# Stick-breaking attention: low key parts on 128 rows, paired products with v, and an earlier third key projection

## The chip, the core and the metric

The kernel runs on one core of a Trainium2 chip. The core has a matrix engine, TensorE (PE in the profile; its loads of the stationary operand are listed apart as PEld), two elementwise engines, VectorE (DVE) and ScalarE (ACT), the slower GpSimd (POOL), and a sync engine (SP) that issues the DMAs. Matmuls read SBUF and write PSUM, which has eight banks of 128 rows by 512 fp32 numbers. The metric is the device time of one execution, in microseconds (us); the median of several runs counts.

## What is computed

The reference is an encoder of two layers on 512 tokens of width 1024. Each layer has a feed-forward block, a token mixer, a second feed-forward block and a gated embedding. The mixer is what the change touches. It projects its input once (`h @ w_in`) and feeds three branches: a stick-breaking attention of four heads of 64, a gated delta rule of four heads of 128 in chunks of 64 tokens (its queries, keys and values pass a convolution over four tokens and a silu), and a short convolution.

```python
def stick_breaking_attention(q, k, v):
    ...
        z = jnp.einsum('bhqd,bhkd->bhqk', qb, kp) * scale
        mask = jnp.arange(t1)[None, :] < jnp.arange(t0, t1)[:, None]
        log_skip = jnp.where(mask, jax.nn.log_sigmoid(-z), 0.0)
        later = lax.cumsum(log_skip, axis=3, reverse=True) - log_skip
        att = jnp.where(mask, jnp.exp(jax.nn.log_sigmoid(z) + later), 0.0)
        outs.append(jnp.einsum('bhqk,bhkd->bhqd', att, vp))
    ...
def gated_delta_rule_chunked(q, k, v, g, beta):
    ...
    gcum = jnp.cumsum(g, axis=-1)
    decay = jnp.exp(jnp.where(incl, gcum[..., :, None] - gcum[..., None, :], -jnp.inf))
    k_beta = k * beta[..., None]
    m = jnp.where(strict, jnp.einsum('nbhik,nbhjk->nbhij', k_beta, k) * decay, 0.0)
    t_inv = lax.linalg.triangular_solve(eye + m, ...)
    ...
```

## The kernel before

**Precision.** Large products run in fp16 in three matmuls: each operand is split into a high part (a rounded copy, made by ACT) and a low part (the rest, made by DVE). `mm3` (lines 256 to 258) issues high by high, high by low and low by high. `split_part` (lines 139 and 140) splits a weight; `load_cols` fetches 256 columns of a weight matrix by one DMA (line 148) and splits them in two halves. Smaller products run directly in fp32; each such matmul shows two records in the profile.

**Order.** The program is written down in one sequence, and a planner makes from it a fixed order for each engine: what stands earlier goes first, but where by the planner's estimates an instruction isn't ready, a later one that is ready fills the gap. So projections written behind a stage stand among its matmuls. An engine works off its order and waits where an input isn't there. Tiles come from pools with a number of buffers per tag: `psa` has two PSUM banks (`acc`, for projections), `psb` three (`bank`), `psc` three (`bank2`); the tag `cv` has five buffers of 128x512 fp32, for convolved projections and for the attention's `l`; the tag `t2` has six.

**The mixer**, `mix_body`, in the order of the program:

- Lines 600 to 611 project the attention's values (`pv` to `sbv`).
- Lines 613 to 625: `conv` copies a projection from PSUM with the last tap (ACT, line 616) and adds three shifted taps (DVE, line 619). The keys of the delta rule come in four projections, one a head. The first two are made here and convolved (`early`).
- Lines 628 to 679 are the gates' work: the decay `g` and `beta` from eight columns, products for cumulative sums (`pe`, lines 654 to 657), their exponential `eg`, and the decay matrices `E` and `ET` (through `gm`, `pl` and `gd`).
- Lines 706 to 722: the silu of each head's keys, transposes and row sums. The weights of the third and fourth key heads are loaded at the head of the second round (lines 707 and 708), and these heads are projected and convolved there (line 711).
- Lines 739 to 789 form `M` and invert its 16x16 blocks, in many small DVE steps and by way of DRAM.
- Lines 795 to 815 project the attention's queries and keys (`psb`). `qs` and `ks` have one tile of 128 rows for each head. In `qs` the head's own 64 rows hold the high part of the queries and the other 64 the low part; `ks` holds the high part of the keys twice. So one matmul on 128 rows gives high by high and low by high. `kl` holds the low part of the keys on the own 64 rows, two heads to a tile, and the third product is a matmul on 64 rows.
- Lines 820 to 873 are the attention, twelve units (h, kts): head h with the key blocks kts, which are (2, 3), (1,) or (0,). A block k meets the queries from k*128 on: 512 columns for block 0, 384, 256 and 128 for blocks 1 to 3. A unit sets up logits in a bank `zb` (three matmuls a block, lines 830, 834 and 838, the last adding the mask), takes softplus (DVE 844, ACT 845 and 846, DVE 847), splits it (ACT 849, DVE 850), sums it over later keys by matmuls with constant triangles (line 857), takes the exponential (ACT 862), and multiplies by the values in fp32 (line 867). That product goes to 64 of the 128 rows of the bank `pav`, which two heads share. Four such groups of a double block, two groups of block 1 and two of block 0 stand alone; block 0 of heads 0 and 2 comes next to block 1 of heads 1 and 3. When both heads are done, lines 872 and 873 copy `pav` out.
- Lines 876 to 896 are the short convolution's projections (`psh`, `psc`, `psbb`); behind them come the values and queries of the delta rule (`pvv`, `pqq`), its gate (`pz`), the sequence of eight chunks, and the output projection.

Of the kernel before, what the change touches and what calls it, by code (L numbers as in the profile page):

```python
# [9 lines left out]
F16 = mybir.dt.float16  # L10
# [3 lines left out]
ALU = mybir.AluOpType  # L14
# [3 lines left out]
P = 128  # L18
D = 1024
KD = D // P  # L20
S = 512
NT = S // P
# [8 lines left out]
IWS = 1.0 / WS  # L31


class Block:
# [524 lines left out]
    def mix_body(self, i, j, last, pool):  # L559
        nc, ins, xT, x = self.nc, self.ins, self.xT, self.x  # L560
        sm = self.small
        w_in = ins["mix_w_in"][i]

        H, C, NC, G16 = 4, 64, 2 * NT, NT * 4
        halves = [slice(64 * e, 64 * e + 64) for e in range(2)]
        heads = [(hp, e) for hp in range(2) for e in range(2)]
        OFF_Q, OFF_K, OFF_V, OFF_Z, OFF_AB, OFF_SC = 768, 1280, 1792, 2304, 2816, 2824
# [20 lines left out]
        ps = self.bank2("ps_rows", (P, 64))  # L588
# [11 lines left out]
        sbv = pool.tile([P, NT, 256], F32, name="sbv")  # L600
# [12 lines left out]
        def conv(ps, c):  # L613
            a = pool.tile([P, S], F32, name="conv", tag="cv", bufs=5)
            w = lambda tap: cw[:, tap * 12 + c : tap * 12 + c + 1]
            nc.scalar.activation(a, ps, AF.Copy, scale=w(3))
            for tap in (2, 1, 0):
                d = 3 - tap
                nc.vector.scalar_tensor_tensor(
                    a[:, d:], ps[:, : S - d], w(tap), a[:, d:], op0=ALU.mult, op1=ALU.add  # L620
                )
            return a

        w = self.load_cols(w_in, OFF_K)
        early = [conv(self.proj_T(w, xT, e, "pk", self.bank2), 4 + e) for e in range(2)]
# [3 lines left out]
        for c in range(2):  # L629
            for e in range(2):  # L630
                nc.tensor.matmul(
                    pab[halves[e], :, c], self.ident[:, halves[c]], ab[:, :, e::2],
                    start=True, stop=True,
# [15 lines left out]
        nc.scalar.activation(beta, pab[:, :, 2:4], AF.Exp, scale=-1.0)  # L649
        nc.vector.tensor_scalar(beta, beta, 1.0, None, op0=ALU.add)  # L650
        nc.vector.reciprocal(beta, beta)
        g16 = g.rearrange("p n h -> p (n h)")
        pe = self.bank("pe", (P, 4, G16))
        nc.tensor.matmul(pe[:, 0], self.uin, g16, start=True, stop=True)
# [40 lines left out]
        def turn(src, name):  # L695


            pts = [self.bank(name, (P, 4, P)) for _ in range(2)]
            for n in range(NC):
                nc.tensor.transpose(pts[n // 4][:, n % 4], src(n), self.ident)  # L700
            return [(pt, slice(4 * b, 4 * b + 4)) for b, pt in enumerate(pts)]

        def chunks(v):
            return v.rearrange("p (n c) -> p n c", c=C)

        for hp in range(2):
            if hp == 1:
                w = self.load_cols(w_in, OFF_K + 256)
            for e in range(2):
                h = 2 * hp + e  # L710
                a = conv(self.proj_T(w, xT, e, "pk"), 4 + h) if hp else early[e]
                self.silu(kq[h][:, :, 0], chunks(a))
            for pt, ns in turn(lambda n: kq2[hp][:, n, 0].rearrange("p e c -> p (e c)"), "pkt"):
                sq = self.t2("sq", (P, 4, P))
                nc.scalar.activation(sq, pt, AF.Square)
                nc.vector.tensor_reduce(
                    ssk[:, ns, hp], sq, axis=mybir.AxisListType.X, op=ALU.add
                )
                nc.vector.tensor_tensor(
                    kdec[:, ns, hp], pt, bc(eg[:, 1].rearrange("p (n h) -> p n h", h=2)[:, ns, hp]),  # L720
                    op=ALU.mult,
                )
# [18 lines left out]
        for a in range(2):  # L741
            a8 = slice(8 * a, 8 * a + 8)
            pm = self.bank("pm", (P, 4, 2, C))
            for n in range(4):
                for hp, e in heads:
                    ks = kq[2 * hp + e][:, 4 * a + n, 0]
# [47 lines left out]

        qs = pool.tile([P, H, S], F16, name="qs", tag="m4", bufs=4)
        ks = pool.tile([P, H, S], F16, name="ks", tag="m4", bufs=4)
        kl = self.t2("kl", (P, 2, S), F16)
        rows_of = lambda e: slice(64 * e, 64 * e + 64)
        for hp in range(2):
            ps = self.proj_T(wq, xT, hp, "psb")  # L800
            for e in range(2):
                own, other, h = rows_of(e), rows_of(1 - e), 2 * hp + e
# [4 lines left out]
        for hp in range(2):  # L807
            ps = self.proj_T(wk, xT, hp, "psb")
            for e in range(2):
                own, other, h = rows_of(e), rows_of(1 - e), 2 * hp + e  # L810
                nc.scalar.activation(ks[own, h], ps[own], AF.Copy, scale=IWS)
                nc.vector.tensor_copy(ks[other, h], ks[own, h])
                nc.vector.scalar_tensor_tensor(
                    kl[own, hp], ps[own], IWS, ks[own, h], op0=ALU.mult, op1=ALU.subtract
                )
        mT = self.act.tile([P, 2, KD, S], F16, name="mT", tag="xT", bufs=2)
        hlb = self.w1.tile([P, 4, 2, 512], F16, name="hl", tag="w")
        pav, hls = [None] * 2, [[None] * NT for _ in range(H)]

        for n_u, (h, kts) in enumerate(((0, (2, 3)), (0, (1,)), (1, (2, 3)), (0, (0,)), (1, (1,)), (2, (2, 3)),  # L820
                       (1, (0,)), (2, (1,)), (3, (2, 3)), (2, (0,)), (3, (1,)), (3, (0,)))):
            hp, e = divmod(h, 2)
            es = slice(64 * e, 64 * e + 64)
            off = {k: 256 * (k == 3) for k in kts}
            n = 512 if kts == (0,) else 384
            zb = self.bank2("zb")[:, :n]
            zt = {k: zb[:, off[k] : off[k] + S - k * P] for k in kts}
            for k in kts:
                kc = slice(k * P, (k + 1) * P)
                nc.tensor.matmul(  # L830
                    zt[k], ks[:, h, kc], qs[:, h, k * P :],
                    start=k == kts[0], stop=False, skip_group_check=True,
                )
                nc.tensor.matmul(
                    zt[k], kl[es, hp, kc], qs[es, h, k * P :], start=False, stop=False,
                    skip_group_check=True,
                )
                nc.tensor.matmul(
                    zt[k][:, :P], self.identb, self.later, start=False, stop=False,
                    skip_group_check=True,  # L840
                )
            l = pool.tile([P, 512], F32, name="sp", tag="cv", bufs=5)[:, :n]

            nc.vector.tensor_scalar(l, zb, 40.0, None, op0=ALU.min)
            self.after(nc.scalar.activation(l, l, AF.Exp), tables)
            nc.scalar.activation(l, l, AF.Ln, bias=1.0)
            nc.vector.tensor_tensor(l, zb, l, op=ALU.max)
            pair = hlb[:, n_u % 4]
            nc.scalar.activation(pair[:, 0, :n], l, AF.Copy)
            nc.vector.tensor_tensor(pair[:, 1, :n], l, pair[:, 0, :n], op=ALU.subtract)  # L850
            for k in kts:
                hls[h][k] = pair[:, :, off[k] : off[k] + S - k * P]
            for k in reversed(kts):
                for k2 in range(NT - 1, k - 1, -1):
                    lhs = self.ntri if k2 == k else self.nones
                    for q in range(2):
                        nc.tensor.matmul(
                            zt[k][:, (k2 - k) * P :], lhs, hls[h][k2][:, q], start=False,
                            stop=k2 == k and q == 1, skip_group_check=True,
                        )  # L860
            at = l
            self.tables_end = nc.scalar.activation(at, zb, AF.Exp)
            if e == 0 and kts[0] == 2:
                pav[hp] = self.bank2("pav")
            for k in kts:
                a0 = at[:, off[k] : off[k] + S - k * P]
                nc.tensor.matmul(
                    pav[hp][es, k * P :], sbv[:, k, 64 * h : 64 * h + 64], a0,
                    start=k == 2, stop=k == 0, skip_group_check=True,
                )  # L870
            if e == 1 and kts == (0,):
                nc.scalar.activation(mT[:, 0, hp], pav[hp], AF.Copy)
                nc.vector.tensor_tensor(mT[:, 1, hp], pav[hp], mT[:, 0, hp], op=ALU.subtract)

# [2 lines left out]
        hb, a = ([self.t2(n) for _ in range(2)] for n in ("hb", "sca"))  # L877
        for c in range(2):
            nc.scalar.activation(hb[c], self.proj_T(wh, xT, c, "psh"), AF.Copy, scale=IWS)
        for c in range(2):  # L880
# [3 lines left out]
            w = lambda tap: cw[:, 48 + 2 * tap + c : 49 + 2 * tap + c]  # L884
# [53 lines left out]
        for hp in range(2):  # L938
            w = self.load_cols(w_in, OFF_V + 256 * hp)
            pair = self.w1.tile([P, NC, 2, C], F32, name="vp", tag="w")  # L940
            for e in range(2):
                next(level, None)
                a = conv(self.proj_T(w, xT, e, "pvv"), 8 + 2 * hp + e)
# [6 lines left out]
        for hp in range(2):  # L950
            w = self.load_cols(w_in, OFF_Q + 256 * hp)
            for e in range(2):
                h = 2 * hp + e
                next(level, None)
                a = conv(self.proj_T(w, xT, e, "pqq"), h)
# [11 lines left out]
        for a in range(2):  # L967
            a8 = slice(8 * a, 8 * a + 8)
            pm = self.bank("pqk", (P, 4, 2, C))
            for n in range(4):  # L970
                for hp, e in heads:
                    k, q = (kq[2 * hp + e][:, 4 * a + n, s] for s in range(2))
# [7 lines left out]
        for hp in range(2):  # L980
            w = self.load_cols(w_in, OFF_Z + 256 * hp)
# [192 lines left out]
```

## Time and profile before

| | |
|---|---|
| median of three runs | 2020.03 us (2019.24 to 2020.5) |
| the profiled execution | 2017.74 us |
| its span in the profile | 2016.0 us |
| granted TensorE clock | 0.996 |
| mixer of the first layer | about 342 to 600 us of the span |
| attention of the first layer | 411.8 to 476.2 us |
| attention of the second layer | 1408.4 to 1472.8 us |

The profile shows one execution. The span runs from the first to the last instruction; the execution's own time has some 1.7 us around it. In a row of the timeline stand the start in us, the length, the engine, the line of the kernel, the operation, what it writes and reads, the form, and the number of merged instructions; in brackets stands how long the engine was idle before, and what released it. The form of a matmul gives the rows and columns of the array in use (64*128 is 64 rows and 128 columns), then the moving operand. The length of a matmul covers its way through the array, so lengths overlap, and the cost of one in a stream is the distance from its start to the next start. A weight load's row (PEld) stands apart from its matmul.

### The profile page before, as it was taken

What the parts mean: (1) busy time and instruction counts of PE and PEld (TensorE: products, weight loads), DVE (VectorE), ACT (ScalarE), POOL (GpSimd) and SP (SyncE); (2) the same over time, 40 slices, a digit from 0 to 9 for tenths busy, and PEclk for the clock granted to TensorE, in tenths of its full rate; (3) what the DMA queues carried; (4) which work ended last, traced back from release to release, by engine and by line L of the source; (5) the groups of instructions that cost most, each with busy time, mean ns of one, the idle gap of its engine ahead of it and who ended that gap; (6) DMA issues with size and microseconds to landing.
All of it is one profiled execution on the core that took longest, in us unless ns stands there. A gap on an engine that the chain in (4) does not pass through costs nothing.

```text
span 2016.0 us, 33100 instructions
## 1 busy us (share of the span) xinstructions
PE 1966.5 (98%) x14058; PEld 1274.0 (63%) x14058; DVE 1524.1 (76%) x2347; ACT 871.4 (43%) x1295; POOL 65.7 (3%) x84
## 2 busy tenths in 40 slices
PE   7999999999999999999999999999999999999998
PEld 5677686544545686776467685854455466776853
DVE  7995866765679895958897877577656797967586
ACT  6453452444345353444264453424544354443431
POOL 1000000100000000000000000001000000000000
PEclk9999999999999999999999999999999999999999
DMA  7543320420253543334224343212222624433221
GB/s 217 189 118 105 105 85 1 127 57 22 84 177 97 155 117 105 105 105 146 106 84 126 105 125 87 62 63 69 53 65 70 201 71 152 113 105 84 95 74 42
DMA packets 245359, 205.15 MB, mean 102 GB/s; under 512 B 20846, under 2 KB 225500, under 8 KB 245212
## 3 DMA queue, kind: packets, MB, share of 16 engines
q1 hardware_dynamic: 245212, 203.05, 33.1%
q8 instruction: 110, 1.80, 0.4%
q14 instruction: 37, 0.30, 0.0%
HBM read 200.14 MB, written 2.88 MB: 101 GB/s over the span
## 4 chain that ended last, share of the span: by engine, by line
PE 74%; DVE 14%; ACT 7%; DMA 2%; issue 2%; SPq 1%; POOL 0%; DVEq 0%; ACTq 0%
PE po L258 7%; PE po L256 7%; PE po L257 7%; PE pA L256 6%; PE pA L257 6%; PE pA L258 6%; DVE w L140 3%; PE pB L258 3%; PE pB L257 3%; PE pB L256 3%; DVE wq L140 2%; ACT w L139 2%; ACT wq L139 2%; PE pC L258 1%; PE pC L257 1%
## 5 line engine op out<-in xcount | busy, mean ns | idle before, releaser
L140 DVE SCALAR_TENSOR_TENSOR wq<-f,wq 128x1024 f16<-128x1024 f32 (+1 forms) x240 | 333.9, 1394 | 19.0 <-ACT wq L139 15.7
L139 ACT ACTIVATE wq<-f 128x1024 f16<-128x1024 f32 (+1 forms) x240 | 279.5, 1191 | 126.0 <-PE pB L258 83.2
L139 ACT ACTIVATE w<-raw 128x1024 f16<-128x1024 f32 (+1 forms) x196 | 193.8, 1031 | 268.2 <-PE po L258 226.1
L256 PE MATMUL po<-w,hT 128*128 128x512 f16 x704 | 266.7, 379 | 3.0 <-ACT hT L286 0.9
L256 PE MATMUL pA<-xS,wq 128*128 128x256 f16 x960 | 261.6, 273 | 6.9 <-ACT up L407 5.5
L257 PE MATMUL po<-w,hT 128*128 128x512 f16 x704 | 266.5, 379 | 0.0
L258 PE MATMUL po<-w,hT 128*128 128x512 f16 x704 | 264.3, 379 | 1.9 <-DVE hT L287 1.9
L258 PE MATMUL pA<-xS,wq 128*128 128x256 f16 x960 | 261.7, 273 | 0.0
L257 PE MATMUL pA<-xS,wq 128*128 128x256 f16 x960 | 261.6, 273 | 0.0
L140 DVE SCALAR_TENSOR_TENSOR w<-raw,w 128x1024 f16<-128x1024 f32 (+1 forms) x196 | 229.4, 1193 | 37.4 <-ACT w L139 37.4
L257 PEld LDWEIGHTS <-wq 128*128 128x128 f16 x2240 | 219.1, 98 | 42.3 <-issue 12.0
L453 DVE TENSOR_TENSOR f<-f 128x512 f32<-128x512 f32 x320 | 218.4, 686 | 27.6 <-DMA f<-in_ffn_w_in 22.5
L256 PEld LDWEIGHTS <-wq 128*128 128x128 f16 x2240 | 219.1, 98 | 30.1
L258 PEld LDWEIGHTS <-wq 128*128 128x128 f16 x2240 | 219.1, 98 | 27.4
L472 DVE SCALAR_TENSOR_TENSOR x_tok<-po,x_tok 128x512 f32<-128x512 f32 x144 | 97.4, 684 | 81.9 <-PE po L258 81.8
L395 DVE TENSOR_TENSOR sg<-pB,sg 128x256 f32<-128x256 f32 x80 | 33.7, 421 | 117.5 <-PE pB L258 117.5
L256 PEld LDWEIGHTS <-hT 128*128 128x128 f16 x704 | 68.8, 98 | 84.7 <-ACT hT L286 9.4
L258 PEld LDWEIGHTS <-hT 128*128 128x128 f16 x704 | 68.0, 98 | 84.8 <-DVE hT L287 5.3
L257 PEld LDWEIGHTS <-hT 128*128 128x128 f16 x704 | 68.9, 98 | 76.7 <-issue 1.2
L392 ACT ACTIVATE sg<-pA 128x256 f32<-128x256 f32 x80 | 30.6, 382 | 194.1 <-PE pA L258 194.1
L257 PEld LDWEIGHTS <-w 128*128 128x128 f16 x640 | 62.7, 98 | 66.0 <-issue 18.0
L258 PEld LDWEIGHTS <-w 128*128 128x128 f16 x640 | 62.8, 98 | 60.3 <-issue 7.2
(289 smaller groups left out, 3836.9 us busy)
## 6 DMA issues: line engine op xcount, KB each, us to landing
f<-in_ffn_w_in SPq DMA_DIRECT2D x160, 512.0 KB, 5.1
raw<-in_ffn_w_out SPq DMA_DIRECT2D x44, 1024.0 KB, 6.0
raw<-in_mix_w_in SPq DMA_DIRECT2D x28, 1024.0 KB, 5.7
raw<-in_mix_w_out SPq DMA_DIRECT2D x8, 1024.0 KB, 4.8
raw<-in_ple_w_gate SPq DMA_DIRECT2D x8, 1024.0 KB, 6.2
raw<-in_ffn_w_in SPq DMA_DIRECT2D x6, 1024.0 KB, 5.8
ln_gb<-in_ln_g SPq DMA_DIRECT2D x8, 512.0 KB, 3.8
ln_gb<-in_ln_b SPq DMA_DIRECT2D x8, 512.0 KB, 4.9
```

The source lines that it names most:

```text
L139: self.nc.scalar.activation(hi, raw, AF.Copy, scale=WS),
L140: self.nc.vector.scalar_tensor_tensor(lo, raw, WS, hi, op0=ALU.mult, op1=ALU.subtract),
L256: nc.tensor.matmul(ps, a[0], b[0], start=first, stop=False, **k)
L257: nc.tensor.matmul(ps, a[0], b[1], start=False, stop=False, **k)
L258: nc.tensor.matmul(ps, a[1], b[0], start=False, stop=last, **k)
L392: nc.scalar.activation(half(new.sg, 1), new.A, AF.Copy)
L395: nc.vector.tensor_tensor(half(old.sg, 1), old.B, half(old.sg, 1), op=ALU.add)
L453: nc.vector.tensor_tensor(f[:, to], f[:, a], f[:, b], op=ALU.add)
L472: self.nc.vector.scalar_tensor_tensor(xs, po, scale, xs, op0=ALU.mult, op1=ALU.add)
```

## The change

Three parts of the mixer are edited. The low parts of the keys get a tile of 128 rows for each head, with the other head's rows set to zero by GpSimd, and their matmul runs on all 128 rows. The products with v are no longer issued unit by unit: the first head of a pair keeps its weights (`weighed`) until the second head has the same key blocks, and then the matmuls of both are issued in turn, with an order set between the two. The bank `pav` is taken at the first such pair. The third key projection, with its load and its convolution, is issued behind `beta` and ahead of `pe`; only the fourth remains in the loop.

```diff
@@ -649,6 +649,8 @@
         nc.scalar.activation(beta, pab[:, :, 2:4], AF.Exp, scale=-1.0)
         nc.vector.tensor_scalar(beta, beta, 1.0, None, op0=ALU.add)
         nc.vector.reciprocal(beta, beta)
+        w = self.load_cols(w_in, OFF_K + 256)
+        early.append(conv(self.proj_T(w, xT, 0, "pk"), 6))
         g16 = g.rearrange("p n h -> p (n h)")
         pe = self.bank("pe", (P, 4, G16))
         nc.tensor.matmul(pe[:, 0], self.uin, g16, start=True, stop=True)
@@ -704,11 +706,9 @@
         for hp in range(2):
-            if hp == 1:
-                w = self.load_cols(w_in, OFF_K + 256)
             for e in range(2):
                 h = 2 * hp + e
-                a = conv(self.proj_T(w, xT, e, "pk"), 4 + h) if hp else early[e]
+                a = conv(self.proj_T(w, xT, e, "pk"), 4 + h) if h == 3 else early[h]
                 self.silu(kq[h][:, :, 0], chunks(a))
@@ -794,7 +794,7 @@
-        kl = self.t2("kl", (P, 2, S), F16)
+        kl = pool.tile([P, H, S], F16, name="kl")
@@ -811,11 +811,12 @@
                 nc.scalar.activation(ks[own, h], ps[own], AF.Copy, scale=IWS)
                 nc.vector.tensor_copy(ks[other, h], ks[own, h])
                 nc.vector.scalar_tensor_tensor(
-                    kl[own, hp], ps[own], IWS, ks[own, h], op0=ALU.mult, op1=ALU.subtract
-                )
+                    kl[own, h], ps[own], IWS, ks[own, h], op0=ALU.mult, op1=ALU.subtract
+                )
+                nc.gpsimd.memset(kl[other, h], 0.0)
@@ -832,7 +833,7 @@
                 nc.tensor.matmul(
-                    zt[k], kl[es, hp, kc], qs[es, h, k * P :], start=False, stop=False,
+                    zt[k], kl[:, h, kc], qs[:, h, k * P :], start=False, stop=False,
                     skip_group_check=True,
                 )
@@ -860,15 +861,22 @@
             at = l
             self.tables_end = nc.scalar.activation(at, zb, AF.Exp)
-            if e == 0 and kts[0] == 2:
+
+            weighed[h, kts] = at
+            if e == 0:
+                continue
+            if kts[0] == 2:
                 pav[hp] = self.bank2("pav")
             for k in kts:
-                a0 = at[:, off[k] : off[k] + S - k * P]
-                nc.tensor.matmul(
-                    pav[hp][es, k * P :], sbv[:, k, 64 * h : 64 * h + 64], a0,
-                    start=k == 2, stop=k == 0, skip_group_check=True,
-                )
-            if e == 1 and kts == (0,):
+                mms = [
+                    nc.tensor.matmul(
+                        pav[hp][halves[h2 % 2], k * P :], sbv[:, k, 64 * h2 : 64 * h2 + 64],
+                        weighed[h2, kts][:, off[k] : off[k] + S - k * P],
+                        start=k == 2, stop=k == 0, skip_group_check=True,
+                    ) for h2 in (h, h - 1)
+                ]
+                self.after(mms[1], mms[0])
+            if kts == (0,):
                 nc.scalar.activation(mT[:, 0, hp], pav[hp], AF.Copy)
                 nc.vector.tensor_tensor(mT[:, 1, hp], pav[hp], mT[:, 0, hp], op=ALU.subtract)
```

More of the change, by code (lines that the diff above doesn't have):

```diff
@@ L813, in mix_body @@
                 nc.vector.scalar_tensor_tensor(
-                    kl[own, hp], ps[own], IWS, ks[own, h], op0=ALU.mult, op1=ALU.subtract
+                    kl[own, h], ps[own], IWS, ks[own, h], op0=ALU.mult, op1=ALU.subtract
                 )
+                nc.gpsimd.memset(kl[other, h], 0.0)
         mT = self.act.tile([P, 2, KD, S], F16, name="mT", tag="xT", bufs=2)
         hlb = self.w1.tile([P, 4, 2, 512], F16, name="hl", tag="w")
-        pav, hls = [None] * 2, [[None] * NT for _ in range(H)]
+        pav, hls, weighed = [None] * 2, [[None] * NT for _ in range(H)], {}
         for n_u, (h, kts) in enumerate(((0, (2, 3)), (0, (1,)), (1, (2, 3)), (0, (0,)), (1, (1,)), (2, (2, 3)),
```

## The prediction, made before the changed kernel ran

> **What bounds the kernel now.** The page comes first: its rows of busy time, then its chain that ended last.
>
> ```profile
> PE 1966.5 (98%) x14058; PEld 1274.0 (63%) x14058; DVE 1524.1 (76%) x2347; ACT 871.4 (43%) x1295; POOL 65.7 (3%) x84
> PE 74%; DVE 14%; ACT 7%; DMA 2%; issue 2%; SPq 1%; POOL 0%; DVEq 0%; ACTq 0%
> ```
>
> TensorE (PE) is covered for 98% of the span and carries 74% of the chain. A covered PE needn't be working at its peak, so the next view is that of windows, over the attention of each layer, from its first product for `zb` to the copy of its last `pav`.
>
> ```profile
> 411.80:476.20 64.40, 63.34 (x348) 28.65 (x347) 41.43 (x82) 33.39 (x60) 0.00 (x0) 1.00 0.17 42
> 1408.40:1472.80 64.40, 63.33 (x348) 28.61 (x347) 41.38 (x82) 33.39 (x60) 0.00 (x0) 1.00 0.17 42
> ```
>
> The columns are length, then PE, PEld, DVE, ACT and POOL busy, the granted clock, and DMA. The two layers are alike. PE is covered for 63.3 of 64.4 us; DVE has 23 us and ACT 31 us to spare. The view of waits names what PE stood for (engine, line, releaser: total, times, longest), in the first layer's mixer, 340 to 600 us:
>
> ```profile
> PE pe L654 <- DVE g L646: 1.6, 1, 1.6
> PE psb L256 <- DVE qs L804: 1.0, 1, 1.0
> ...
> PE zb L857 <- ACT hl L849: 0.8, 1, 0.8
> ```
>
> Only the last lies in the attention. The softplus chains on DVE and ACT are covered, because projections (`psh`, `psc`, `psbb`) fill PE meanwhile. So this stage ends when PE has issued its work, and time that PE doesn't need is time saved, as long as the cover lasts.
>
> **The low parts of the keys (L834).** What does a 512-column fp16 matmul cost in an undisturbed stream? The timeline of PE has nine steps between these two:
>
> ```profile
> 422.19 0.38 PE L258 MATMUL psh<-xT,w 128*128 128x512 f16 x1
> ...
> 424.13 0.38 PE L258 MATMUL psh<-xT,w 128*128 128x512 f16 x1
> ```
>
> 1.94 / 9 = 0.216 us from start to start (the 0.38 is a length with its pipeline, and overlaps). Now a 512-column unit of the attention, and the matmul that follows it:
>
> ```profile
> 428.39 0.38 PE L830 MATMUL zb<-qs,ks 128*128 128x512 f16 x1
> 428.70 0.39 PE L834 MATMUL zb<-qs,kl 64*128 64x512 f16 x1
> 429.02 0.23 PE L838 MATMUL zb<-later,identb 128*128 128x128 bf16 x1
> 429.08 0.38 PE L256 MATMUL psh<-xT,w 128*128 128x512 f16 x1
> ```
>
> From L830 to L838 pass 0.63 us, where two such matmuls need 0.43. The 0.20 too much lies in equal parts before and behind the one matmul on 64 rows; L838 (bf16, 128 rows) and the fp16 behind it are only 0.06 apart, so it isn't the type. With `kl` on 128 rows all three have one form. The added rows multiply zeros and no column is added, so the matmul itself should keep its 0.216.
>
> ```profile
> L834 PE MATMUL zb<-qs,kl x32: 226/306/387, 412.0 to 1465.6; 64*128 64x256 f16 x8, 64*128 64x128 f16 x8, 64*128 64x384 f16 x8, 64*128 64x512 f16 x8
> ```
>
> 32 x 0.20 = **6.4 us**, all of it on PE's path. The bounds are 0 (the gap has another reason) and 6.4. DVE's L813 keeps its shape. GpSimd gets four memsets of 64x512 f16 a layer:
>
> ```profile
> 367.77 1.80 POOL L782 MEMSET TU<- 128x2048 f32 x1 [16.91 <-DVE w L140]
> 396.96 2.91 POOL L732 TENSOR_TENSOR rk<-ssk,mhalf 128x16 f32<-128x16 f32 x1 [27.39 <-DVE ssk L724]
> ```
>
> Each has a quarter of that memset's columns in half its type, so four stay under 7.2 us, in 27.4 us in which POOL is idle. I count nothing. Without that cover L732 would be late behind them, and with it the M chain, which PE's psb projections hide.
>
> **The products with v (L867).** The timeline shows each group with the instruction that follows it: a double block alone, a 384 alone, a 512 alone, and the two groups in which two heads already met.
>
> ```profile
> 419.71 0.86 PE L867 MATMUL pav<-sp,sbv 128*64 128x256 f32 x4
> 420.51 0.34 PE L830 MATMUL zb<-qs,ks 128*128 128x384 f16 x1
> ...
> 427.31 0.86 PE L867 MATMUL pav<-sp,sbv 128*64 128x384 f32 x2
> 428.10 0.23 PE L857 MATMUL zb<-hl,nones 128*128 128x128 f16 x1
> ...
> 435.52 0.38 PE L258 MATMUL psc<-xT,w 128*128 128x512 f16 x1
> 435.87 1.25 PE L867 MATMUL pav<-sp,sbv 128*64 128x512 f32 x4
> 437.05 0.28 PE L830 MATMUL zb<-qs,ks 128*128 128x256 f16 x1
> ...
> 467.49 1.19 PE L867 MATMUL pav<-sp,sbv 128*64 128x512 f32 x4
> 468.61 0.39 PE L830 MATMUL zb<-qs,ks 128*128 128x512 f16 x1
> ...
> 475.14 1.07 PE L867 MATMUL pav<-sp,sbv 128*64 128x512 f32 x2
> 476.14 0.39 PE L257 MATMUL pvv<-xT,w 128*128 128x512 f16 x1
> ```
>
> From start to the next start: 0.80 for (2,3) alone, 0.79 for (1) alone, 1.00 for (0) alone; an fp32 product has two records, which I call passes. A merged row names only its first form: the two mixed groups hold a 512 of one head and a 384 of the other, and take 1.18 and 1.12 instead of 1.79 in turn. Per layer: 4 x 0.80 + 2 x 0.79 + 2 x 1.00 + 1.18 + 1.12 = 9.08 us.
>
> Do two heads overlap from the start? In the mixed groups the second came late for want of data:
>
> ```profile
> 435.21 0.99 ACT L862 ACTIVATE sp<-zb 128x512 f32<-128x512 f32 x2 [0.51 <-PE zb L857]
> ```
>
> Two exponentials end at 436.20; the first allowed the start at 435.87, the second head had to wait. The groups by form, from 467.50 to 467.95 in the second mixed group, show who had begun:
>
> ```profile
> L867 PE MATMUL pav<-sp,sbv 128*64 128x512 f32 x1 | 0.6, 643 | 0.0
> L867 PE MATMUL pav<-sp,sbv 128*64 128x384 f32 x1 | 0.5, 537 | 0.0
> ```
>
> One pass of each head and not yet the 512's second: the other head ran beside it, in the same bank, in the other 64 columns. So I let a pair cost what one head costs alone: 2 x (0.80 + 0.79 + 1.00) = 5.18 us a layer, 3.90 less, **7.8 us** in two layers. Four groups fewer also save entries (bounded in the first rival below); counted as nothing. The new edge between the two matmuls of a pair stays on one engine.
>
> The added wait: head h-1's products stand until head h has its weights, so their `l` buffers (five, under the tag `cv`) are held longer. Behind an L844 without a buffer DVE queues softplus and conv steps, and PE's L857 waits for those. By the order of units at most two are held beside those in work; between 0 and the 0.8 us wait above per unit, I take 0.
>
> In return `pav` is first needed after three units instead of one. At 420.51 the second unit's `zb` starts right behind the first product; if that order of the three banks is the reason, units will overlap more. It shortens a chain that PE hides: nothing counted.
>
> **The third key projection.** It is written ahead of `pe`, with its load and split; on the sync queue the load keeps its place between the first keys' and wq's. What did the chip do so far?
>
> ```profile
> 370.86 0.39 PE L257 MATMUL pk<-xT,w 128*128 128x512 f16 x1
> ...
> 374.97 0.38 PE L258 MATMUL pk<-xT,w 128*128 128x512 f16 x1
> 376.93 0.37 PE L654 MATMUL pe<-g,uin 128*128 128x16 f32 x2 [1.58 <-DVE g L646]
> ```
>
> The first two rows bound the third projection: it already runs there, and PE then stands for `g`. DVE in that time, ACT's copy for the third conv, and the conv's first steps:
>
> ```profile
> 375.39 0.17 DVE L645 SCALAR_TENSOR_TENSOR g<-g,spa 128x16 f32<-128x16 f32 x1 [0.23 <-ACT spa L644]
> 375.49 1.22 DVE L140 SCALAR_TENSOR_TENSOR w<-raw,w 128x1024 f16<-128x1024 f32 x1
> 376.62 0.17 DVE L646 TENSOR_TENSOR g<-g,nega 128x16 f32<-128x16 f32 x1
> ...
> 378.66 0.69 ACT L616 ACTIVATE conv<-pk,cw 128x512 f32<-128x512 f32 x1 [0.43 <-PE pk L258]
> ...
> 379.39 1.53 DVE L619 SCALAR_TENSOR_TENSOR conv<-pk,cw,conv 128x511 f32<-128x511 f32 x2 [0.35 <-ACT conv L616]
> ```
>
> A split of 1.22 us stands between the two steps of `g`. What the edit moves is the conv: ACT's copy ahead of `eg`, and three DVE steps (1.5 for two, so 2.2 us) ahead of `gc` and the decay tiles. Bounds a layer: the 1.6 us stand vanishes, or `pe` waits 2.2 us longer. `g` stays ahead of the conv in the program and the projections behind `pe` cover what comes later, so I take **0**; what would be late next is `gm` for L672, in the middle of the fourth projection.
>
> **Sum.** 6.4 + 7.8 + 0 = 14.2 us. The profiled execution lasted 2017.74 us (span 2016.0), so 2003.5 in its terms. The three timed runs have their median at 2020.03, 2.3 us above; the steps are the same in both, so I take 14.2 from the median: **2005.8 us**.
>
> **Rivals.**
> *More than the sum.* The conv, ready earlier, takes the place of the split and the 1.6 us stand goes in both layers (3.2), and the entries of four groups a layer go too. An entry is the 0.35 from the last projection's matmul at 435.52 to 435.87, less 0.22: 0.13 x 8 = 1.0. That gives 2001.6. Against it: something of 0.6 us or more will stand beside `g` on DVE anyhow. 10%.
>
> *Products overlap only in part.* If a pass couldn't start before all passes ahead of it in the program, the second head's first pass would run beside the first head's second. From 0.79 and 1.00, 128 more columns in two passes cost 0.21, so a 512 pass has 0.42 and a group 0.16 around. Pairs would take 3 x 0.42 + 0.16 = 1.42, 3 x 0.315 + 0.16 = 1.11, and 4 x 0.21 + 0.16 = 1.00 instead of 2.59 in all: 0.94 more, four times, 3.8 us: 2009.6. The two rows by form speak against it. 8%. The Trainium skill states this rule in "TensorE: Matmul & The Clock Gate", section "The mechanism": "MATMULs are pc-monotone in start AND end". By it the time would be 2009.6; the trace doesn't agree, since by 467.95 the 384 had begun and the 512's second pass hadn't.
>
> *The rows aren't the reason for the gaps at L834.* Then 6.4 us stay: 2012.2. Every L834 has both gaps and its neighbours of one form have none; 5%.
>
> *PE meets the chain (the slower side).* PE's order is fixed beforehand. With 14.2 us less of its own work it reaches each unit's first L857, or the paired product, before ACT and DVE are done, as it did once a layer (0.8 us). There are 24 units: at 14.2 / 24 = 0.59 us a unit all is given back; at 0.8 us 19.2 are lost and the time is 2025.0, slower. For it: products already follow their exponentials closely. Against it: DVE and ACT are a third to a half idle, and a shorter product also starts the next chain earlier. 6% for that, 6% for 0.43 to 0.75 a unit (within 0.2%), 9% for about 0.3 a unit (7.2 given back, 2013.0).
>
> **How the numbers follow.** 56% for the sum itself, 2003 to 2009 with small shifts of waits; 10 + 8 + 5 + 9% for the other faster cases. The range takes them in, from 2001.0 to 2013.0, about eight in ten. A measurement of this kernel tells about 0.2%, 4.0 us, from no change: faster 0.88, same 0.06, slower 0.06.
>
> **What will show it.** The `kl` matmuls as 128*128, 0.22 us behind a 512-column L830 and 0.22 before L838; three groups of products per pair of heads, 0.80, 0.79 and 1.00 long with both heads in them; an attention some 7 us shorter in each layer, with PE as covered as now; `pe` still waiting 1 to 2 us for `g`. I am wrong if the waits of PE for L849 or L862 grow to several us a layer, if a pair lasts as long as two heads, or if the time saved in the attention comes back behind it as a wait for weights or for the chunks' chain.

## The result, and the profile after

| | before | after |
|---|---|---|
| median beside each other | 2019.63 us (4 runs, 2017.52 to 2020.5) | 2003.6 us (4 runs, 2002.96 to 2004.63) |
| ratio, 95% interval | | 0.9927 [0.9915, 0.9939] |
| profiled execution | 2017.74 us | 2003.89 us |
| its span | 2016.0 us | 2002.2 us |

The kernel is faster by 16.0 us in the medians and by 13.85 us in the two profiled executions. The sum of the prediction was 14.2 us. The question left is whether it is made of the parts that the sum has. First comes the row of busy time of the profile's page, after:

```profile
PE 1951.1 (97%) x14058; PEld 1271.2 (63%) x14058; DVE 1522.9 (76%) x2347; ACT 870.6 (43%) x1295; POOL 69.9 (3%) x92
```

PE has the same number of matmuls and 15.4 us less cover. Now PE's timeline, after: the first pair of products and the 512-column unit behind it, then a pair of 384 and a pair of 512 columns.

```profile
426.00 0.38 PE L258 MATMUL psh<-xT,w 128*128 128x512 f16 x1
426.31 0.87 PE L872 MATMUL pav<-sp,sbv 128*64 128x256 f32 x8
427.12 0.39 PE L831 MATMUL zb<-qs,ks 128*128 128x512 f16 x1
427.34 0.38 PE L835 MATMUL zb<-qs,kl 128*128 128x512 f16 x1
427.56 0.22 PE L839 MATMUL zb<-later,identb 128*128 128x128 bf16 x1
427.61 0.33 PE L831 MATMUL zb<-qs,ks 128*128 128x384 f16 x1
...
434.44 0.87 PE L872 MATMUL pav<-sp,sbv 128*64 128x384 f32 x4
435.24 0.23 PE L839 MATMUL zb<-later,identb 128*128 128x128 bf16 x1
...
442.93 1.08 PE L872 MATMUL pav<-sp,sbv 128*64 128x512 f32 x4
443.94 0.28 PE L831 MATMUL zb<-qs,ks 128*128 128x256 f16 x1
```

The low-part matmul (L835) now starts 0.22 us behind L831, and L839 starts 0.22 behind it: 0.44 from L831 to L839, where it was 0.63. The first pair holds eight records instead of four and takes 427.12 - 426.31 = 0.81, the others 0.80 and 1.01: a pair costs what one head cost. So both mechanisms work as foreseen. Yet the attention did not become 7 us shorter. The view of windows, from the first product for `zb` to the first one for `pu`, a product of the delta rule's chunks (the same matmuls in every kernel), in both layers, before and then after:

```profile
411.82:479.26 67.44, 66.38 (x361) 29.87 (x359) 42.10 (x83) 33.99 (x61) 0.00 (x0) 1.00 0.16 40
1408.44:1475.89 67.45, 66.38 (x361) 29.86 (x359) 42.03 (x83) 33.99 (x61) 0.00 (x0) 1.00 0.16 40
```

```profile
411.60:473.32 61.72, 59.58 (x361) 28.67 (x359) 41.87 (x87) 33.43 (x61) 0.00 (x0) 1.00 0.17 43
1400.18:1461.92 61.74, 59.58 (x361) 28.68 (x360) 41.87 (x87) 33.43 (x61) 0.00 (x0) 1.00 0.18 43
```

The stretch is shorter by 5.72 and 5.71 us (length, first number behind the times), but PE's cover in it (second number) by 6.80. PE was uncovered for 1.06 us of it, and now for 2.14. The largest waits of PE ahead of the attention and in it, first layer, after the change; then the rows of the timeline around two of the three at L858:

```profile
PE pe L656 <- DVE g L646: 1.3, 1, 1.3
PE psb L256 <- DVE qs L804: 1.3, 1, 1.3
PE zb L858 <- ACT hl L850: 1.2, 1, 1.2
...
PE zb L858 <- DVE sp L848: 0.4, 1, 0.4
PE zb L858 <- DVE hl L851: 0.4, 1, 0.4
```

```profile
414.81 0.38 PE L256 MATMUL psh<-xT,w 128*128 128x512 f16 x1
416.43 0.22 PE L858 MATMUL zb<-hl,ntri 128*128 128x128 f16 x1 [1.25 <-ACT hl L850]
...
417.35 0.38 PE L258 MATMUL psh<-xT,w 128*128 128x512 f16 x1
418.10 0.22 PE L858 MATMUL zb<-hl,ntri 128*128 128x128 f16 x1 [0.38 <-DVE hl L851]
```

The same place in the kernel before:

```profile
416.14 0.38 PE L257 MATMUL psh<-xT,w 128*128 128x512 f16 x1
417.30 0.22 PE L857 MATMUL zb<-hl,ntri 128*128 128x128 f16 x1 [0.78 <-ACT hl L849]
```

Such a wait of PE is called a stand here. It is best measured between starts, as lengths overlap: 416.43 - 414.81 = 1.62, less the 0.216 of the projection's own matmul, is 1.41 after; before it was 0.94. The new kernel has three stands above 0.25 us in the stretch (1.41, then 0.54 from 417.35 and 0.54 at 422.16), all ahead of the sums of early units; before there were two (0.94 and one of 0.27). So 2.49 us a layer are spent standing, and 1.21 were.

That gives an account for each layer: the stretch is PE's stands above 0.25 us and a rest, which is PE's work with its small gaps.

| kernel | stretch | stands | rest |
|---|---|---|---|
| before | 67.44 | 1.21 | 66.23 |
| after | 61.72 | 2.49 | 59.24 |

(The last digits are rounded.) The rest fell by 6.99 us a layer; the sum had (6.4 + 7.8) / 2 = 7.1. The stands gave 1.28 of it back. Over two layers 11.43 us came from this stretch. The other 2.4 of the 13.85 were gained in one place that the sum didn't have: the second layer between the attention's values (`pv`) and the first `zb`, 2.33 us shorter, where the first layer's same part is unchanged (0.03 us). What lies there shows in the windows of the kernel before, with the granted clock as the third number from the end, and then after, both in the projection behind `pe`:

```profile
1374.00:1376.00 2.00, 2.00 (x6) 0.74 (x5) 1.04 (x3) 0.69 (x1) 0.00 (x0) 0.50 0.87 211
```

```profile
1368.00:1370.00 2.00, 2.00 (x10) 0.78 (x8) 2.00 (x5) 0.00 (x0) 0.00 (x0) 1.00 0.94 293
```

In the profiled execution of the kernel before, the granted clock was halved for 3.41 us from 1373.06 on, just behind PE's stand for `g`, and six matmuls lie in these 2 us instead of ten. In the one of the changed kernel it wasn't halved there.

### The profile page after: what moved, and what is told of

Read it like the earlier page. It is cut to its first block, busy times and chain, and to the rows that moved or that the text cites. A ratio compares the mean times of both kernels' runs of the same rounds, so it can differ in the third digit from the quotient of the medians.

```text
span 2002.2 us, 33105 instructions
## 1 busy us (share of the span) xinstructions
PE 1951.1 (97%) x14058; PEld 1271.2 (63%) x14058; DVE 1522.9 (76%) x2347; ACT 870.6 (43%) x1295; POOL 69.9 (3%) x92
## 4 chain that ended last, share of the span: by engine, by line
PE 73%; DVE 15%; ACT 7%; issue 2%; DMA 2%; SPq 1%; POOL 0%; DVEq 0%; ACTq 0%
PE po L258 7%; PE po L256 7%; PE po L257 7%; PE pA L256 6%; PE pA L258 6%; PE pA L257 6%; DVE w L140 3%; PE pB L258 3%; PE pB L257 3%; PE pB L256 3%; DVE wq L140 2%; ACT w L139 2%; ACT wq L139 2%; PE pC L256 1%; PE pC L258 1%
## 5 line engine op out<-in xcount | busy, mean ns | idle before, releaser
L257 PEld LDWEIGHTS <-w 128*128 128x128 f16 x640 | 62.6, 98 | 67.0 <-issue 19.4
L223 ACT ACTIVATE xT<-ps_t 128x512 f16<-128x512 f32 x64 | 35.4, 594 | 150.6 <-PE ps_t L220 150.4
```

The costliest lines, as they stand in the source:

```text
L223: nc.scalar.activation(hi, ps, AF.Copy),
L257: nc.tensor.matmul(ps, a[0], b[1], start=False, stop=False, **k)
```

## The experiments

The theory after this comparison: both parts remove the PE work that was reckoned, and what is missing is PE standing for the softplus chain of the first units. Rivals: one of the parts is worth less work than reckoned; the missing time lies elsewhere. Each run is compared with runs of the kernel before that were made beside it (their medians are 2018.1, 2016.51 and 2019.66 us in the three groups). Those runs reach from 2015.2 to 2021.7 us, so small differences are read from the stretch above, which in these profiles differs by at most 0.21 us from the first layer to the second.

**One part alone.** The kernel before, with only the hunks of the low parts (1), of the products (2), or of the third projection (3):

```diff
 (1)
+        kl = pool.tile([P, H, S], F16, name="kl")
...
+                nc.gpsimd.memset(kl[other, h], 0.0)
...
+                    zt[k], kl[:, h, kc], qs[:, h, k * P :], start=False, stop=False,
 (2)
+            weighed[h, kts] = at
+            if e == 0:
+                continue
...
+                    ) for h2 in (h, h - 1)
 (3)
+        w = self.load_cols(w_in, OFF_K + 256)
+        early.append(conv(self.proj_T(w, xT, 0, "pk"), 6))
...
```

(1) 

> The kernel before with only the low key parts on 128 rows. By the theory of the row form: the gaps of 0.10 us on both sides of each of the 32 matmuls go, 6.4 us, so about 2013.2 on a before of 2019.6; a little less (2014) if PE meets the softplus chain. By the rival that the gaps have another reason: 2019.6, and the gaps stay in the trace.

(2) 

> The kernel before with only the paired products with v. Full overlap: 7.8 us of PE work go; after the extra waits ahead of the first unit's sums that the changed kernel showed (some 1.3 us a layer) about 5.2 us remain: 2014.4. Partial overlap (a second head's first pass only beside the first head's second): 3.8 us less gain, 2018. If the waits come from the pairs' edit, they are here; if they come from the faster logits, they are in the run with kl alone.

(3) 

> The kernel before with only the third key projection moved. By the landmarks of the two traces: 0 in the first layer, 2.3 us in the second, where the wait for the decay shrinks and the stretch at a lower clock behind it goes: 2017.0 to 2017.5. If those 2.3 us of the second layer are chance of one profile: 2019.6.

| kernel | median, us (runs) | ratio to before | stretch (layer 1) | stands | rest |
|---|---|---|---|---|---|
| (1) low parts | 2014.47 (11) | 0.9985 [0.9976, 0.9993] | 65.97 | 2.97 | 63.00 |
| (2) products | 2006.06 (5) | 0.9943 [0.9930, 0.9956] | 62.24 | 0 | 62.24 |
| (3) third projection | 2016.69 (12) | 0.9998 [0.9989, 1.0008] | 67.44 | 1.20 | 66.23 |

The windows of (1) and then of (2) show the same by the cover:

```profile
413.89:479.85 65.96, 63.61 (x361) 29.98 (x360) 42.45 (x86) 34.36 (x61) 0.00 (x0) 1.00 0.16 41
```

```profile
411.17:473.41 62.24, 62.12 (x361) 28.42 (x359) 41.01 (x83) 33.56 (x61) 0.00 (x0) 1.00 0.17 43
```

In (1) the rest falls by 3.23 us (reckoned 3.2), but the stands grow by 1.76, and only 1.47 us a layer are left (1.69 in the second). In (2) the rest falls by 3.99 (reckoned 3.90) and all stands go too: 5.20 a layer, twice what was expected of this run. With products needed only after the second head, three units' logits go out at the start (2.31 us of PE, where one unit's took 0.86), and PE has enough to do while the first chain runs. So both works are sized right, and the stands decide how much of them is won. The third projection alone changes nothing that can be measured. In its profile the clock is halved in the second layer too (from 1372.17 on), and from the last `pv` matmul to the first `zb` pass 53.04 us there, 53.06 in the kernel before and 50.72 in the changed one: the 2.33 us can't be put down to this edit. (2) alone has most of the gain.

**The changed kernel without the rows.** Only the hunks (1) undone:

> The changed kernel with only the low parts of the keys back on 64 rows, thus the pairs and the third projection together. If the parts add as the runs of one part alone say (pairs 5.2 us a layer, rows 0.5 on top): stretch 134.0 us a layer, time 2004.5 to 2006.5. If the rows are worth their 3.2 us a layer once the pairs are there: stretch 136 to 137, time near 2010.

It took 2006.57 us (5 runs), ratio 0.9935 [0.9922, 0.9947]:

```profile
411.94:474.18 62.24, 62.12 (x361) 28.44 (x359) 40.99 (x83) 33.55 (x61) 0.00 (x0) 1.00 0.18 43
```

62.24 of stretch with no stand, as in (2). The rows take the rest from 62.24 to 59.24, 3.00 us, of which 2.49 turn into stands: 0.52 us a layer remain. On the kernel before they gave 1.47 to 1.69, so the two parts don't add; the products give 5.20 with or without the third projection.

**What do the stands wait for?** VectorE has the 16x16 blocks to invert at that time. Its timeline after, ahead of the first unit's softplus:

```profile
412.66 0.20 DVE L770 TENSOR_TENSOR prod<-mb,X 128x25 f32<-128x25 f32 x1
412.90 0.18 DVE L774 TENSOR_REDUCE X<-prod 128x5 f32<-128x25 f32 x1
413.12 0.22 DVE L770 TENSOR_TENSOR prod<-mb,X 128x36 f32<-128x36 f32 x1
413.37 0.56 DVE L845 TENSOR_SCALAR sp<-zb 128x384 f32<-128x384 f32 x1
```

Steps of the inverse (L770 and L774) go on until the softplus begins at 413.37, though the first unit's logits went out from 411.60 on. The first attempt wrote the inverse behind the attention loop, once with the low parts on 128 rows and once on 64:

```diff
-        X = self.t2("X", (P, 2, 16, 16))
...
-        for r in range(1, 16):
...
+        X = self.t2("X", (P, 2, 16, 16))
...
+        for r in range(1, 16):
...
         wh, wc, wb = ahead[2:] + [self.load_cols(w_in, OFF_SC)]
```

> The changed kernel, but the 15 steps of the block inverse (its small products and sums on DVE, and the DMAs behind them) stand behind the attention in the program, so that they give way to the softplus chains. Theory: the changed kernel's waits ahead of the first units' sums, 2.5 us a layer, come from the first softplus step standing behind such steps on DVE; then they go: 4 to 5 us less, 1999 to 2000. Rival: the chain of ACT and DVE itself is too long for what the planner puts between; then the waits stay and it takes 2003 to 2004. If the inverse comes too late for the stage that uses it, a wait appears there and it is slower.

> The kernel with the inverse behind the attention, but the low key parts back on 64 rows. Theory: with the waits gone the row form is worth its full 6.4 us, so 6 us more than the kernel beside it. Rival (the row form was worth little on top of the pairs because its gaps lay in time that PE waited for anyway): 1 us more, as between the changed kernel and the pairs alone.

It took 2004.38 us (5 runs), 0.9934 [0.9922, 0.9946], stretch 61.99 with stands of 1.63 and 0.94; on 64 rows 2008.71 us (6), 0.9952 [0.9939, 0.9965], stretch 63.39 with stands of 0.59 and 0.53. Both expectations missed, but the trace shows that the edit did not move the steps that matter: eleven of them still run ahead of the first softplus, as many as in the changed kernel. So the first of them was tied behind the second unit's low part:

```diff
-            nc.vector.tensor_tensor(pair[:, 1, :n], l, pair[:, 0, :n], op=ALU.subtract)
+            low = nc.vector.tensor_tensor(pair[:, 1, :n], l, pair[:, 0, :n], op=ALU.subtract)
+            if n_u == 1:
+                second = low
...
+            if r == 1:
+                self.after(step, second)
```

> The changed kernel with the block-inverse steps behind the attention loop in program, and the first of them tied behind the second softplus unit's low part on the same engine, so that they stand behind the first units' chain on VectorE for certain (with the place alone eleven of them still stood in front). Theory (the missing 1.4 us of the two edits in each layer are TensorE standing for the first units' chain, which VectorE reaches late because of the inverse): the stand of 1.4 us before the first unit's sums shrinks to under 0.5 and the stretch from the first zb matmul to the first pot is 132 to 132.8 us a layer instead of 133.5; time 2001.5 to 2003. Rival (the chain is late by its own length, or the inverse is late for its own reader afterwards): stretch 133.3 to 134, time 2003.5 to 2005.

> The same with the low parts of the keys back on 64 rows. Theory: with the stands gone the rows are worth their 3.2 us of TensorE time a layer, so the stretch is 135 to 136 us a layer and the time 6 us above the run with 128 rows. Rival (the rows' saving ends in a stand whatever VectorE does): stretch 134 to 134.8, time 1 to 3 us above.

DVE, and then the sums of two units on PE, with 128 rows (here L819 is the first softplus step and L834 the sums):

```profile
412.86 0.56 DVE L819 TENSOR_SCALAR sp<-zb 128x384 f32<-128x384 f32 x1 [1.23 <-PE zb L813]
```

```profile
415.42 0.38 PE L256 MATMUL psh<-xT,w 128*128 128x512 f16 x1
416.16 0.22 PE L834 MATMUL zb<-hl,ntri 128*128 128x128 f16 x1 [0.35 <-ACT hl L824]
...
430.34 0.38 PE L257 MATMUL psc<-xT,w 128*128 128x512 f16 x1
431.35 0.38 PE L834 MATMUL zb<-hl,nones 128*128 128x128 f16 x3 [0.63 <-DVE sp L822]
```

From the first logits to the first softplus step pass 412.86 - 412.21 = 0.65 us instead of 413.37 - 411.60 = 1.77, and the first stand falls from 1.41 to 0.52. The expectation for this stand just failed (under 0.5), the one for the length held: 132.70 us to the first `pot`, where the changed kernel has 133.48. So the inverse did hold up the first chain. But a new stand of 0.79 came at 430.34, so that of 2.49 us of stands 1.90 are left; and the median, 2004.94 us, lies in the rival's range and not in the 2001.5 to 2003 of the theory.

| kernel | median, us (5 runs each) | ratio to before | stretch | stands | rest |
|---|---|---|---|---|---|
| 128 rows | 2004.94 | 0.9926 [0.9912, 0.9940] | 60.93 | 1.90 | 59.03 |
| 64 rows | 2006.67 | 0.9936 [0.9924, 0.9948] | 62.61 | 0.93 | 61.68 |

The rows are now worth 1.68 us a layer instead of 0.52, and 1.7 us for both layers in the medians. On 64 rows the length to the first `pot` is 134.37, in the rival's range: where the inverse gives way, the rest differs by 2.65 us and the stands take back 0.97 of it, about a third. The stretch of 60.93 is the shortest of all kernels, but the time (2001.47 to 2007.72) can't be told from the changed kernel's, and none was measured to be faster than that.

Another cause was not tested. PE's order fixes how many of the projection's matmuls stand between the early logits and the first sums: 17 in the kernel before, 16 in (2) and in the changed kernel with 64 rows, 10 in the changed kernel and in both kernels of the last table. Six of them are 1.30 us, nearly the first stand of 1.41. The first pair of products starts 14.71 us into the stretch in the changed kernel, behind 42 such matmuls, and 14.78 us into it with 64 rows, behind 48. So PE had projections left that could have filled the stand; whether more of them in that place would have kept the rows' gain, with VectorE left as it is, stays open.

**The bank of `pav`.** The prediction held the order of three banks responsible for the logits that now go out early. Taking the bank ahead of the first pair:

```diff
             if e == 0:
+                if kts[0] == 2:
+                    pav[hp] = self.bank2("pav")
                 continue
-            if kts[0] == 2:
-                pav[hp] = self.bank2("pav")
```

> The changed kernel, but the bank of the products is taken after the first unit of a pair, as before, instead of after the third. If the 1.3 us a layer of new waits come from three units crowding at the start of the attention, they go and it takes 2001 (2.6 less than 2003.6). If instead the single-file units of before come back and cost, 2004 to 2008. Same work on PE in both.

It took 2004.15 us (6 runs), 0.9930 [0.9918, 0.9942], stretch 61.71. PE's order came out the same as in the changed kernel, so nothing is learned about the bank: that three units go out because the bank is free stays an argument.

**Is the alternation needed?** One head's two products, then the other's:

```diff
+            for h2 in (h, h - 1):
+                for k in kts:
...
-                self.after(mms[1], mms[0])
```

> The changed kernel with the pair's matmuls not in turn: both key blocks of one head, then both of the other. Only the double blocks differ, four pairs in all. If the matrix engine starts a later matmul in free columns over two waiting ones, the same time, 2003.6, and the double group stays 0.80 us. If it sees only the next one: the second head starts beside the first head's last block, the group takes about 1.1 us, and 1.2 us are added in all.

It took 2004.54 us (5 runs), 0.9935 [0.9923, 0.9947], stretch 61.73. The first pair in PE's timeline, and the groups by form between 426.85 and 426.95:

```profile
426.86 0.88 PE L872 MATMUL pav<-sp,sbv 128*64 128x256 f32 x8
427.67 0.39 PE L831 MATMUL zb<-qs,ks 128*128 128x512 f16 x1
```

```profile
L872 PE MATMUL pav<-sp,sbv 128*64 128x256 f32 x2 | 0.4, 430 | 0.0
```

The pair again takes 0.81. Within 0.1 us two 256-column passes have begun and no 128-column one, though the program now has the first head's 128-column product between the two heads' 256. The second head starts 0.013 us behind the first, where it was 0.007 in the changed kernel. So the second head's product began ahead of matmuls that stand in front of it in the program; the planner's own order at this place isn't shown by the trace. Issuing the heads in turn isn't what makes the overlap; it is enough that two heads' products stand next to each other.

**The wait for `g`.** Its last step given to GpSimd:

```diff
-        nc.vector.tensor_tensor(
+        nc.gpsimd.tensor_tensor(
             g, g, nega.rearrange("p (a h) -> p a h", a=1).to_broadcast([P, NC, 2]), op=ALU.mult
```

> The changed kernel with the second step of the decay (times the negative rate) on GpSimd instead of DVE, where it stands behind a weight's split. The wait for it, 1.3 and 0.6 us in the two layers, should fall to 0.3 or less: 1 to 1.5 us less, 2002.3. If something else on DVE is late next, no change.

It took 2004.6 us (6 runs), 0.9937 [0.9923, 0.9951]. The wait got longer, not shorter as expected, in the first layer's mixer:

```profile
PE pe L656 <- POOL g L646: 1.4, 1, 1.4
```

In its profile the clock was halved at 379.7 and, for 6.83 us, at 1369.5, behind stands of 1.55 and 2.14 us. So this run says nothing on what the stand costs alone.

## Why the prediction was right, and where its working was not

It said 2005.8 us, 2001.0 to 2013.0, faster; it was 2003.6. Step by step:

- **Low parts: the work held, the gain didn't.** The gaps at L834 went as read from the timeline; alone, the rest of the stretch fell by 3.23 us a layer for 3.2 reckoned. But "all of it on PE's path" was the step that failed. Alone the edit gave 1.5 to 1.7 us a layer, on top of the products 0.52, because PE, done sooner with what its order puts ahead of the first sums, then stood for the first units. The inverse on DVE was shown to be one cause of that; the few projections in that place are another, untested.
- **Products: held.** 0.81, 0.80 and 1.01 for a pair, from 0.80, 0.79 and 1.00 for one head. The work fell by 3.99 us a layer (3.90 reckoned). The early logits, counted as nothing, came with the end of the 1.21 us of stands while the rows were on 64, so that alone the edit gave 5.20.
- **Third projection: held at nothing.** Alone 0.9998 [0.9989, 1.0008]. `pe` still waits, 1.3 us in the first layer as foreseen, but 0.6 in the second, where 1 to 2 were foreseen.
- **The sum.** 14.0 us of the 14.2 of PE's work went; 2.6 came back as stands; 2.3 were gained in the second layer ahead of the attention. The total of the profiles, 13.85, is close to 14.2 because these two nearly cancel, not because every gain was full. Most of the 2.3 is a halved clock that the one execution had and the other hadn't (1.5 to 1.7 us), the other part a shorter stand for `g` (1.89 us before, 0.77 after, in layer two). So the closeness to 14.2 is in part luck. Against the other medians of the kernel before (2016.51 to 2019.66) the gain is 12.9 to 16.1 us; its size is known no better than that.
- **The rivals.** "PE meets the chain" happened, at a small size and in another form: not in 24 units, but at three places among the early ones of each layer, 1.28 us a layer more, far from the 0.59 a unit at which all is lost. It was seen in the row that the prediction quoted (0.8 us for L849) and in the phrase "as long as the cover lasts", but its chances were priced as a like amount in every unit, from 0.3 us on. The partial overlap (2009.6) is out: its 1.11, 1.00 and 1.42 us for a pair stand against 0.81, 0.80 and 1.01. By the Trainium skill's rule in "TensorE: Matmul & The Clock Gate", section "The mechanism", matmuls start in program order. Both traces of pairs disagree: the second head's first pass starts 0.007 us (written in turn, 0.013) behind the first head's, whose own second pass starts 0.27 us behind its first.
- **Memsets on GpSimd** cost nothing that shows: after them no wait of PE in the mixer names POOL.

## What to carry to other kernels

Time taken from an engine that is "covered" is won only where the engine's next input is there; look at the start of a stage, where little other work has been put ahead, for the chain that was hidden until now, and count in the new order what stands ahead of the first wait. Two edits that draw on the same cover needn't add: the rows gave 1.5 to 1.7 us a layer alone and 0.52 on top of the products, so measure each alone and on top of the other. And where an order is planned from estimates, look in the trace at what was moved before an experiment's theory is called refuted.

## What the runs showed of the hardware

**A matmul on 64 rows among matmuls on 128 cost a gap on each side.** It is 0.10 us ahead and 0.10 behind each of 32 such matmuls; with 128 rows, half of them zeros, both are gone.

**Two fp32 products that write different halves of a bank's rows ran beside each other.** A pair took 0.81, 0.80 and 1.01 us where one alone took 0.80, 0.79 and 1.00.

**A stand of 1.4 to 2.4 us may halve the clock, or not.** The thirteen profiles have 26 stands ahead of `pe`. None of the eight shorter than 1.3 us was followed by a halved clock; of the eighteen from 1.34 to 2.40 us eight were, for 3.41 us (once 6.83). For the same stand in the same kernel it can come in one layer and not in the other:

```profile
1372.09 0.37 PE L654 MATMUL pe<-g,uin 128*128 128x16 f32 x2 [1.73 <-DVE g L646]
...
1374.15 0.63 PE L256 MATMUL pk<-xT,w 128*128 128x512 f16 x1
1374.58 0.63 PE L257 MATMUL pk<-xT,w 128*128 128x512 f16 x1
```

These rows are of the kernel before, second layer: 0.43 us from start to start, where 0.216 is usual. In the first layer a stand of 1.75 us went by without it. The stretch from `pe` to `zb` is then 1.5 to 1.7 us longer. In each trace the changes of the clock lie whole multiples of 3.413 us apart (in the kernel before those at 38.45, 1373.06 and 1376.47 by 391 and by 1). Cut at these steps, each of the eight halvings begins at the end of the 3.413 us that hold the most of the stand, 1.31 to 2.17 us of it. The stand of 1.75 us is divided by such an end, with 1.18 us on the longer side. It isn't the whole condition: five other stands have 1.32 to 1.67 us on one side and no halving. That the clock follows a window of time that runs on its own is what the Trainium skill states ("TensorE: Matmul & The Clock Gate", section "What's actually happening": 4096 cycles, 3413 ns); the 3.413 us agree. The same section of the Trainium skill has the clock fall after at least one idle window. The eight halvings don't fit that, since the longest of the 26 stands is 2.40 us. How much of the spread of the kernel before, 2015.2 to 2021.7 us, is due to it was not counted, as only profiled executions show the clock.
